# A hybrid attention layer on one core: the first softmax item a unit later, squares on ScalarE, three more short products

## The chip, the cores and the metric

The kernel runs on one core of a Trainium2 chip. A core has five engines that work through queues of their own, each in order: TensorE (PE, matrix products and transposes), VectorE (DVE), ScalarE (ACT), GpSimd (POOL) and SyncE (SP, which issues the loads). The metric is the device time of one execution in microseconds (us).

## The reference

One decoder layer for 256 positions and 1024 channels, all in float32. Two token mixers read one projection of the normalised input; their gated sum is projected and added to x; then a second norm and a gated feed-forward network with a causal convolution.

```
h = rmsnorm(x, g_mix)
q_a, kv_a, gate_a, qkv_b, merge = split(h @ w_in)          # 1024 x 5656
kc, vc = compress(...)                                     # small MLP with gelu over blocks of keys, values
o_a = nsa_attention(q_a, kc, vc, ks, vs, kw, vw, gate_a)   # 8 heads: compressed, selected, window
o_b = dilated_attention(qkv_b)                             # 12 heads in 3 groups
mixed = sigmoid(g_A) * (o_a @ w_proj_nsa) + sigmoid(g_B) * (o_b @ w_proj_dil)
x = x + mixed @ w_out
h = x * rsqrt(mean(x * x) + eps) * g_ffn                   # the second norm
x = x + (gelu(conv(h @ w_u)) * (h @ w_gate)) @ w_down
return rmsnorm(x, g_final)
```

## The kernel before

**Units.** The weights come in 64 units, mostly of 128 x 2048 float32, one load each into one of three `raw` buffers. A product in float32 is made of three products in a shorter format: ACT copies a unit to its high half `whi` (`split_hi`, L128), DVE subtracts to get the low half `wlo` (`split_lo`, L132), and the moving operand is split in the same way (`hTh`, `hTl`). `parts` (L162) first issues high by high and high by low, product by product (L177), and then low by high (L182): 32 and 16 products of 256 columns in a usual unit. The next load into a raw buffer waits until its low half is made.

**The order** is written out by hand, unit by unit, in the loop at L1094; there is no scheduler. Units 0 to 4 make keys, values and the queries of the first mixer, 5, 7 and 9 queries of the second, 6 and 8 the first layer of the compression MLP (L425), 10 to 15 its keys and values, 16 to 23 the merge gates, 24 to 26 the two projections, 27 to 30 `w_out`, and from unit 31 (`NFIRST`) on the feed-forward network.

**Items.** The softmax of the mixers is cut into items that are spread over the units (`slots`, L1085). An item in slot n makes its scores behind the products of unit n (`qk`, for the first mixer L850 and L852). During unit n+1 DVE adds the penalty and takes the row's extreme (`sm`, L864), ACT takes the exponential and its sum (L869), and DVE scales by one over the sum and a gate (`sm2`, three small operations and L883). Behind unit n+1 PE transposes the scaled scores (`tr`, L892, eight transposes), both engines copy them out (`te`, L897 and L898), and behind unit n+2 they multiply the values (`pv`, L905). Within a unit the loop writes `sm`, then the gelu of the compressed keys (`cmp_gelu`, only in unit 10, L751 to L762), then the low half of the next unit, then `sm2`; in unit 9 alone `sm2` goes ahead of the low half (L1109). The compressed keys are folded behind unit 9 (`cmp_fold`, L745).

**The second norm.** Each of the units 27 to 30 adds a quarter of `w_out`'s result to x (`ev_out`, L552): DVE adds (L555), ACT and DVE split the scaled result for the next products (`split_x`, L201 and L202), and POOL squares it and keeps a running sum of 128 x 2 x 256 (L561, L563), which it folds to `acc2` at the last quarter (L567). The column sums of `acc2` are taken on PE in unit 32 (L209), and the rest of the norm goes into the eviction of the feed-forward products. At unit 31 ACT's queue issues the load of the last gain into memory that the sums have held, so it waits for L567, and the high half of unit 33 stands behind it.

**Short products.** In units 24 and 33 `rt["kick"] = "own"` puts a product of 64 columns in front of the unit (L172), into columns that the first full product overwrites.

Of the kernel before, what the change touches and what calls it, by code (L numbers as in the profile page):

```python
# [14 lines left out]
AF = mybir.ActivationFunctionType  # L15
OP = mybir.AluOpType
# [77 lines left out]
def build(ctx, tc, a, out):  # L94
    nc = tc.nc
    V, A, P, T = nc.vector, nc.scalar, nc.gpsimd, nc.tensor
# [41 lines left out]
    def hi_of(i):  # L138
        if 2 <= i < len(units):
            split_tiles(units[i])  # L140
            (units[i].split or (split_hi, split_lo))[0](units[i])

    def lo_of(i):
        if 2 <= i < len(units):
            if i == 27:
                split_lo(units[i], 1024, 2048, P)
                return
            if i in SHARED:
                split_lo(units[i], 0, SHARED[i])
                split_lo(units[i], SHARED[i], 2048, P)  # L150
                return
            (units[i].split or (split_hi, split_lo))[1](units[i])
# [47 lines left out]
    def split_x(kt, x, g):  # L200
        A.activation(hTh[:, kt], x, AF.Copy, scale=g[:, kt:kt + 1])  # L201
        V.scalar_tensor_tensor(hTl[:, kt], x, g[:, kt:kt + 1], hTh.bitcast(F32)[:, kt],  # L202
                               op0=OP.mult, op1=OP.subtract)
# [45 lines left out]
    def mixer_tiles():  # L249
        M["QS"] = att.tile([128, 8, S], F32R, name="QS", tag="QS")  # L250
        for n in ("qb", "kb"):
            M[n] = att.tile([128, 6, S], F32, name=n, tag=n)
        M["vb"] = att.tile([128, 2, 3, 256], F32, name="vb", tag="vb")
# [3 lines left out]
    rt = {}  # L257
# [45 lines left out]
    def xc_tile():  # L303
        xr["XC"] = att.tile([128, 4, 520], F32R, name="XC", tag="MB")
        for i in range(4):
            V.memset(xr["XC"].bitcast(F32)[:, i, 512:520], 0.0)
# [19 lines left out]
    def split_cmp(i):  # L326
        f, XC = xr["f"][:, 2 * i:2 * i + 2], xr["XC"]
        hi, lo = XC[:, 2 * i:2 * i + 2, 0:256], XC[:, 2 * i:2 * i + 2, 256:512]
        A.activation(hi, f, AF.Copy)
        V.tensor_sub(lo, f, XC.bitcast(F32)[:, 2 * i:2 * i + 2, 0:256])  # L330
# [221 lines left out]
    def ev_out(c):  # L552
        def f(u):
            x = xT[:, 2 * c:2 * c + 2]
            V.tensor_tensor(out=x, in0=x, in1=u.p, op=OP.add)  # L555
            for k in range(2):
                split_x(2 * c + k, xT[:, 2 * c + k], G2)
            if c == 0:
                rt["sqs"] = att.tile([128, 4, 2, S], F32, name="sqs", tag="MA")
            sq = rt["sqs"][:, c]  # L560
            P.tensor_tensor(out=sq, in0=x, in1=x, op=OP.mult)  # L561
            if c:
                P.tensor_tensor(out=sq, in0=sq, in1=rt["sq"], op=OP.add)  # L563
            rt["sq"] = sq
            if c == 3:
                rt["acc2"] = const.tile([128, S], F32, name="acc2")
                P.tensor_tensor(out=rt["acc2"], in0=sq[:, 0], in1=sq[:, 1], op=OP.add)  # L567
        return f

    for c in range(4):  # L570
        units.append(Unit(2048, mm_out(c), ev_out(c)))
# [87 lines left out]
    NFIRST = len(units)  # L659
# [73 lines left out]
    def cmp_sum():  # L733

        S2 = att.tile([64, 2, 128], F32, name="S2", tag="c1")
        p = rt["ph"][0:64]
        A.activation(S2, p[:, :, 0], AF.Copy)
        V.tensor_tensor(out=S2, in0=p[:, :, 1], in1=S2, op=OP.add)
        cmp_["S2"] = S2
# [7 lines left out]
    def cmp_gelu():  # L747

        w = att.tile([128, 3, 64], F32, name="gl")
        x, y, e = w[:, 0], w[:, 1], w[:, 2]  # L750
        A.activation(x, cmp_["cm"][:, 0:64], AF.Copy)  # L751
        V.tensor_tensor(out=y, in0=x, in1=x, op=OP.mult)
        V.tensor_scalar(y, y, 0.044715, 1.0, op0=OP.mult, op1=OP.add)
        V.tensor_tensor(out=y, in0=y, in1=x, op=OP.mult)
        V.tensor_scalar(y, y, -50.0, None, op0=OP.max)
        A.activation(e, y, AF.Exp, scale=-2.0 * float(np.sqrt(2.0 / np.pi)))
        V.tensor_scalar(e, e, 1.0, None, op0=OP.add)
        V.reciprocal(e, e)
        hk = att.tile([128, 32], F32, name="hk")
        hv = att.tile([128, 4, 32], F32, name="hv")  # L760
        V.tensor_tensor(out=hk, in0=x[:, 0:32], in1=e[:, 0:32], op=OP.mult)
        V.tensor_tensor(out=hv, in0=x[:, None, 32:64].to_broadcast([128, 4, 32]),  # L762
                        in1=e[:, None, 32:64].to_broadcast([128, 4, 32]), op=OP.mult)
        cmp_["hk"], cmp_["hv"] = hk, hv
# [249 lines left out]
    def load_to(n):  # L1014
        nonlocal loaded
        while loaded < min(n, len(units)):
            load_unit(units[loaded])
            loaded += 1
# [63 lines left out]
    tables_pool3()  # L1082

    items = {11: [Cmp()]}
    slots = [8, 10] + list(range(12, 22))  # L1085
    seq = [c(h, t) for c in (Nsa, Dil) for q in (0, 2) for h, t in (((q,), 1), ((q + 1,), 1), ((q, q + 1), 0))]
    for n, it in zip(slots, seq):
        items.setdefault(n, []).append(it)
# [1 line left out]
    def at(i):  # L1090
        return items.get(i, [])

    post = []
    for i, u in enumerate(units):  # L1094
        load_to(i + LA)
        if i == 9:
            cmp_sum()
        for it in at(i - 3):
            it.fin()
        for it in at(i - 2):  # L1100
            it.te()
        for it in at(i - 1):
            it.sm()
        if i == 10:
            cmp_gelu()
        if i == 2:
            hi_of(3)
            lo_of(3)
        if i == 9:  # L1109
            for it in at(i - 1):  # L1110
                it.sm2()
        if i > 2:
            lo_of(i + 1)
        if i != 9:
            for it in at(i - 1):
                it.sm2()
        if i == 14:
            nc.sync.dma_start(xT, a["xT"])
        if i == 3:
            hi_of(5)  # L1120
            mixer_tiles()
            xc_tile()
            split_cmp(0)
            split_cmp(1)
            u1.evac(u1)
        if i == 4:
            split_keys()
        if i == 11:
            cmp_kv_ev()
        if i == 14:  # L1130

            ob = att.tile([128, 4, S], F32R, name="ob", tag="qa")
            OB.update(h=ob[:, 0:2], l=ob[:, 2:4])
        if i in (23, 24):
            m = ML[i - 23]
            A.activation(m, m, AF.Sigmoid)
        if i == NFIRST:
            st.close()
            ffn["pool"] = ctx.enter_context(tc.tile_pool(name="ffn", bufs=1))
            gf = ffn["pool"].tile([128, D], F32, name="gf")  # L1140
            nc.scalar.dma_start(gf, bass.AP(tensor=a["g_final"].tensor, offset=a["g_final"].offset,
                                            ap=[[0, 128], [1, D]]))
            X = ffn["pool"].tile([128, 2, D], F32, name="X")
            sq = ffn["pool"].tile([128, 512], F32, name="sq")
        if 24 <= i <= 25:
            hi_of(i + 2)
        if i in (24, NFIRST + 2):
            rt["kick"] = "own"
        u.mm(u)
        if not 24 <= i <= 26 and i > 1 and i != 3:  # L1150
            hi_of(i + 2)
        if i == 2:
            u0.evac(u0)
        if i == NFIRST + 1:
            rt["R2"] = rows_of(rt["rs2"], "R2", "o")
            units[NFIRST].evac(units[NFIRST])
            ps2 = pd([2, 512], "s")
            pt = [pd([512], "t"), pd([512], "t"), ps2[:, 0], ps2[:, 1]]
            for q in range(4):
                for c in range(4):  # L1160
                    T.transpose(pt[q][:, c * 128:c * 128 + 128], xT[:, 4 * (q % 2) + c, q // 2 * 128:q // 2 * 128 + 128],
                                ident)
            for q in range(4):
                A.activation(X[:, q // 2, q % 2 * 512:q % 2 * 512 + 512], pt[q], AF.Copy)
        if post:
            post.pop()()
        if u.pre:
            u.pre(u)
        if u.evac and i not in (0, 1, NFIRST):
            u.evac(u)  # L1170
        if i in (6, 7):
            q_parts(i - 6)
        if i == 7:
            gates_of()
        if u.pre:
            post.append(post_g(len([q for q in units[:i] if q.pre])))
        for it in at(i - 2):
            it.pv()
        for it in at(i - 1):
            it.tr()  # L1180
        for it in at(i):
            it.qk()
        if i == 9:
            cmp_fold()
        if i == 10:
            cmp_kv()
# [34 lines left out]
    x = X[:, 1, 768:1024]  # L1221
# [28 lines left out]
```

## Time and profile before

| | us |
|---|---|
| median of 3 executions (406.04 to 407.66) | 406.07 |
| the profiled execution | 406.5 |
| its span, first to last instruction | 404.7 |
| PE busy | 394.7 (98%) |
| DVE busy | 291.2 (72%) |
| ACT busy | 212.4 (52%) |
| POOL busy | 31.2 (8%) |

PE is busy almost all the time, and its granted clock is at full speed from the first slices to the last one of the page. Since a busy PE hides little, the thing to read is where it waits, and what stands in the queue of the engine that it waits for. Ends of products are modelled in the trace, their starts are measured.

### The profile page before, as it was taken

Reading aid. Unit: us, or ns where it says so; the run is one execution under the profiler, and the core shown is the slowest. Engines: PE = TensorE matmul, PEld = TensorE weight load, DVE = VectorE, ACT = ScalarE, POOL = GpSimd, SP = SyncE. Lnnn points to the kernel's source line nnn. Section 1 sums busy time; section 2 is a strip of 40 time slices with the busy share of each in tenths; the row PEclk is TensorE's granted clock in tenths of the full one; section 3 lists DMA queues with packets and bytes.
Section 4 is the critical chain, followed back from the end, with each engine's and each line's share of the span. In section 5 each row is a group of like instructions: output and inputs, shape, how many; then the busy total and the mean of one; then the engine's idle time right before and its main releaser. Section 6 shows DMA issues by size and latency. Waiting matters only on the chain.

```text
span 404.7 us, 8015 instructions
## 1 busy us (share of the span) xinstructions
PE 394.7 (98%) x3412; PEld 383.2 (95%) x3412; DVE 291.2 (72%) x486; ACT 212.4 (52%) x293; POOL 31.2 (8%) x58
## 2 busy tenths in 40 slices
PE   8999989999999999999999999999999999999993
PEld 6999989999998989999999999999999999999992
DVE  5879889887786557458897499676594774946853
ACT  5776764366664345663554765445264352643512
POOL 7100000000000000061143000000000000000012
PEclk9999999999999999999999999999999999999997
DMA  8965746345332532343556346662734726438002
GB/s 319 390 251 207 249 168 209 105 158 220 144 105 105 201 113 105 131 181 108 206 208 235 130 136 236 255 222 108 296 119 194 266 99 261 160 152 299 15 0 105
DMA packets 10980, 72.59 MB, mean 179 GB/s; under 512 B 1216, under 2 KB 1472, under 8 KB 2880
## 3 DMA queue, kind: packets, MB, share of 16 engines
q1 hardware_dynamic: 10512, 70.96, 48.2%
q10 hardware_dynamic: 432, 1.11, 0.7%
q8 instruction: 27, 0.44, 0.4%
q14 instruction: 9, 0.07, 0.1%
HBM read 71.02 MB, written 1.05 MB: 178 GB/s over the span
## 4 chain that ended last, share of the span: by engine, by line
PE 83%; DVE 10%; ACT 2%; DMA 2%; issue 1%; SPq 0%; POOLq 0%; POOL 0%; ACTq 0%
PE ps_d L177 25%; PE ps_d L182 12%; PE ps_o L177 9%; PE ps_s L630 8%; PE ps_t L630 7%; PE ps_o L182 5%; DVE wlo L132 4%; DMA first<-in_first_dram 2%; PE ps_t L177 2%; DVE hTl L202 2%; PE ps_d L344 2%; PE ps_o L905 2%; PE ps_s L946 1%; PE ps_t L892 1%; PE ps_d L280 1%
## 5 line engine op out<-in xcount | busy, mean ns | idle before, releaser
L132 DVE TENSOR_TENSOR wlo<-raw,whi 128x2048 fp32r<-128x2048 f32 (+2 forms) x61 | 135.2, 2217 | 4.2 <-ACT whi L128 4.2
L128 ACT ACTIVATE whi<-raw 128x2048 fp32r<-128x2048 f32 (+1 forms) x61 | 114.8, 1883 | 33.6 <-DMA raw<-in_wts_dram 28.8
L177 PE MATMUL ps_d<-hTh,whi 128*128 128x256 f32 x384 | 90.1, 280 | 0.0
L177 PE MATMUL ps_d<-hTl,whi 128*128 128x256 f32 x384 | 89.0, 277 | 0.0
L177 PEld LDWEIGHTS ps_d<-hTh,whi 128*128 128x128 f32 x384 | 72.2, 188 | 1.7 <-issue 1.3
L177 PEld LDWEIGHTS ps_d<-hTl,whi 128*128 128x128 f32 x384 | 72.2, 188 | 0.0
L182 PE MATMUL ps_d<-hTh,wlo 128*128 128x256 f32 x384 | 47.8, 277 | 0.0
L182 PEld LDWEIGHTS ps_d<-hTh,wlo 128*128 128x128 f32 x384 | 45.7, 188 | 0.0
L177 PE MATMUL ps_o<-hTh,whi 128*128 128x256 f32 x160 | 36.9, 277 | 0.0
L177 PE MATMUL ps_o<-hTl,whi 128*128 128x256 f32 x160 | 36.8, 276 | 0.0
L585 ACT ACTIVATE C<-U,small 128x256 f32<-128x256 f32 x22 | 12.0, 595 | 44.1 <-DVE U L581 44.1
L177 PEld LDWEIGHTS ps_o<-hTl,whi 128*128 128x128 f32 x160 | 30.1, 188 | 0.0
L177 PEld LDWEIGHTS ps_o<-hTh,whi 128*128 128x128 f32 x160 | 30.0, 188 | 0.0
L589 DVE SCALAR_TENSOR_TENSOR C<-U,small,C 128x256 f32<-128x256 f32 x44 | 19.4, 482 | 7.5 <-ACT C L585 7.4
L869 ACT ACTIVATE E<-E,ast 128x256 f32<-128x256 f32 (+1 forms) x32 | 14.2, 444 | 13.4 <-DVE ast L864 13.4
L581 DVE TENSOR_TENSOR U<-ps_d,R 128x512 f32<-128x512 f32 x6 | 4.1, 690 | 23.0 <-PE ps_d L182 19.2
L182 PE MATMUL ps_o<-hTh,wlo 128*128 128x256 f32 x160 | 19.8, 276 | 0.0
L132 POOL TENSOR_TENSOR wlo<-raw,whi 128x1024 fp32r<-128x1024 f32 x3 | 7.7, 2579 | 154.8 <-ACT whi L128 154.8
L182 PEld LDWEIGHTS ps_o<-hTh,wlo 128*128 128x128 f32 x160 | 18.9, 188 | 0.0
L581 DVE TENSOR_TENSOR U<-ps_o,R 128x512 f32<-128x512 f32 x5 | 3.4, 689 | 17.6 <-PE ps_o L182 17.6
L1207 POOL TENSOR_TENSOR tiny<-cst,tiny 128x1 f32<-128x1 f32 x2 | 1.4, 696 | 170.6 <-ACT sq L1206 170.6
L366 DVE TENSOR_TENSOR ML<-ps_d,R 128x512 f32<-128x512 f32 x8 | 5.5, 692 | 12.3 <-PE ps_d L182 12.3
(269 smaller groups left out, 762.5 us busy)
## 6 DMA issues: line engine op xcount, KB each, us to landing
raw<-in_wts_dram SPq DMA_DIRECT2D x61, 1024.0 KB, 4.8
first<-in_first_dram SPq DMA_DIRECT2D x2, 768.0 KB, 8.1
raw<-in_wts_dram SPq DMA_DIRECT2D x1, 1120.0 KB, 11.0
xn<-in_xn_dram SPq DMA_DIRECT2D x2, 512.0 KB, 12.4
xT<-in_xT_dram SPq DMA_DIRECT2D x1, 1024.0 KB, 6.9
first<-in_first_dram SPq DMA_DIRECT2D x2, 384.0 KB, 5.3
gf<-in_g_final_dram ACTq DMA_DIRECT2D x1, 512.0 KB, 3.7
out_dram<-X SPq DMA_DIRECT2D x1, 512.0 KB, 2.6
```

The costliest lines, as they stand in the source:

```text
L128: A.activation(u.hi[:, u.o + c0:u.o + c1], u.raw[:, c0:c1], AF.Copy)
L132: (eng or V).tensor_sub(u.lo[:, u.o + c0:u.o + c1], u.raw[:, c0:c1], u.hi.bitcast(F32)[:, u.o + c0:u.o + c1])
L177: T.matmul(po, l, r, start=start and bank not in banks, stop=False, skip_group_check=True)
L182: T.matmul(po, l, r, start=False, stop=stop and n == len(ks) - 1, skip_group_check=True)
L202: V.scalar_tensor_tensor(hTl[:, kt], x, g[:, kt:kt + 1], hTh.bitcast(F32)[:, kt], op0=OP.mult, op1=OP.subtract)
L344: T.matmul(u.p[:, i], l[:, kt, i * 128:i * 128 + 128], r[:, kt], start=kt == 0 and i == 0 and q == 0, stop=kt == 7 and q == 2, skip_group_ ...
L581: V.tensor_tensor(out=U[:, :, 2:], in0=u.p, in1=bc(rt["R2"], 2), op=OP.mult)
L585: A.activation(C[:, c], U[:, c, 2:], AF.Identity, scale=CW(2, t), bias=CB[:, t:t + 1])
L589: V.scalar_tensor_tensor(C[:, c], U[:, c, w:w + S], CW(w, t), C[:, c], op0=OP.mult, op1=OP.add)
L630: T.matmul(ffn["y"][t][ch][:, b:e] if own is None else own, x[:, kt, t * 128:t * 128 + 128], w[:, kt, ch * 512 + b:ch * 512 + e], start=st ...
L869: A.activation(self.E[:, i], self.E[:, i], AF.Exp, bias=mn[:, i:i + 1], scale=-1.0, accum_out=dn[:, i:i + 1])
L905: T.matmul(oA[js[c]][g * 64:g * 64 + 64, t * 128:(t + 1) * 128], Vn[:, k, b * 128 + g * 64:b * 128 + g * 64 + 64], self.PT[:, i], start=t ...
```

## The change

Three edits. The first item of the first mixer moves from slot 8 to slot 9; all other items stay. The squares of the second norm are made by ACT instead of POOL; POOL keeps the running sum over the first three quarters, folds it to `acc2` at the third, and at the last quarter adds the two halves of that quarter's squares to `acc2`, one after the other. And units 11, 13 and 23 get a short product in front as well.

```diff
             sq = rt["sqs"][:, c]
-            P.tensor_tensor(out=sq, in0=x, in1=x, op=OP.mult)
-            if c:
+            A.activation(sq, x, AF.Square)
+            if c in (1, 2):
                 P.tensor_tensor(out=sq, in0=sq, in1=rt["sq"], op=OP.add)
             rt["sq"] = sq
-            if c == 3:
+            if c == 2:
                 rt["acc2"] = const.tile([128, S], F32, name="acc2")
                 P.tensor_tensor(out=rt["acc2"], in0=sq[:, 0], in1=sq[:, 1], op=OP.add)
+            if c == 3:
+                for k in range(2):
+                    P.tensor_tensor(out=rt["acc2"], in0=rt["acc2"], in1=sq[:, k], op=OP.add)
...
-    slots = [8, 10] + list(range(12, 22))
+    slots = [9, 10] + list(range(12, 22))
...
-        if i in (24, NFIRST + 2):
+        if i in (11, 13, 23, 24, NFIRST + 2):
             rt["kick"] = "own"
```

Lines behind the second edit stand three lines further down in the changed kernel. On PE, before, from the end of unit 8 (L425) to the start of unit 11; the 32 products L177 of each unit are left out. The scores stand ahead of unit 9, the transposes behind it, and `pv` and the second item's scores behind unit 10:

```order
L425 MATMUL ps_d<-wlo,XC 64x256 x8
L850 MATMUL ps_s<-KH,QS 128x512 x2
L852 MATMUL ps_s<-KL,QS 128x512 x2
...
L182 MATMUL ps_d<-hTh,wlo 128x256 x16
L892 MATMUL ps_t<-ident,E 128x128 x8
L745 MATMUL ps_o<-E_142,S_746 128x32 x2
...
L905 MATMUL ps_o<-PT,Vn 64x128 x8
```

And of the change, the same stretch up to the short product of unit 11:

```order
L425 MATMUL ps_d<-wlo,XC 64x256 x8
...
L182 MATMUL ps_d<-hTh,wlo 128x256 x16
L853 MATMUL ps_s<-KH,QS 128x512 x2
L855 MATMUL ps_s<-KL,QS 128x512 x2
L748 MATMUL ps_o<-E_142,S_741 128x32 x2
...
L895 MATMUL ps_t<-ident,E 128x128 x8
...
L772 MATMUL ps_o<-hk,small 64x32 x2
L773 MATMUL ps_o<-small,hv 128x64
L172 MATMUL ps_d<-hTh,whi 128x64
```

The scores moved behind unit 9 and the transposes behind unit 10; `pv` of this item is now behind unit 11.

On DVE, before, the operations of the first item between the compression's sum (L738) and the gelu (L752 on); the four reductions L864 alternate with readings of their accumulators:

```order
L738 TENSOR_TENSOR S_746<-ps_d,S_746 64x256
L864 ISA E,ast<-ps_s,tab 128x256
...
L876 TENSOR_SCALAR ast<-ast 128x4
L877 RECIPROCAL ast<-ast 128x4
L880 TENSOR_TENSOR ast<-ast,gates 128x4
L883 TENSOR_SCALAR E<-E,ast 128x256 x4
L132 TENSOR_TENSOR wlo<-raw,whi 128x2048
L454 SCALAR_TENSOR_TENSOR qb<-ps_d,scB,R 128x256 x2
L898 COPY PT<-ps_t 128x512
L752 TENSOR_TENSOR gl<-gl 128x64
```

Of the change, from the same sum to the scaling:

```order
L741 TENSOR_TENSOR S_741<-ps_d,S_741 64x256
L132 TENSOR_TENSOR wlo<-raw,whi 128x2048
L454 SCALAR_TENSOR_TENSOR qb<-ps_d,scB,R 128x256 x2
L867 ISA E,ast<-ps_s,tab 128x256
...
L755 TENSOR_TENSOR gl<-gl 128x64
...
L765 TENSOR_TENSOR hv<-gl 128x128
L132 TENSOR_TENSOR wlo<-raw,whi 128x2048
L879 TENSOR_SCALAR ast<-ast 128x4
...
L886 TENSOR_SCALAR E<-E,ast 128x256 x4
```

Between the reductions and the scaling now stand the gelu chain of eight operations (L755 to L765) and the low half of unit 11. On ACT the copy that begins the gelu chain (L754, before L751) stands behind the item's four exponentials.

On POOL, the second norm, both orders in one piece; `acc` is `acc2`:

```order
-L561 TENSOR_TENSOR sqs<-xT 128x512
-L563 TENSOR_TENSOR sqs<-sqs 128x512
-L567 TENSOR_TENSOR acc_2583<-sqs 128x256
+L563 TENSOR_TENSOR sqs<-sqs 128x512 x2
+L567 TENSOR_TENSOR acc_2524<-sqs 128x256
+L570 TENSOR_TENSOR acc_2524<-acc_2524,sqs 128x256 x2
 L215 TENSOR_TENSOR tiny<-tiny,cst 128x2
```

The multiplies are gone from POOL, the fold comes ahead of the last quarter, and two adds of 128x256 follow it. Each of the four activations (L561) stands on ACT behind the two copies L201 of its quarter and ahead of the next high half.

## Rows read from the trace of the kernel before

**Rows 1.** Who waited for whom on PE, from 17 to 235 us.
```profile
PE ps_t L892 <- DVE E L883: 0.9, 1, 0.9
PE ps_d L280 <- DVE wlo L132: 0.4, 1, 0.4
```

**Rows 2.** Time line of PE, units 9 and 10: start, length, instructions, [idle before].
```profile
54.74 1.98 PE L182 MATMUL ps_d<-hTh,wlo 128*128 128x256 f32 x16
57.62 1.46 PE L892 MATMUL ps_t<-ident,E 128*128 128x128 f32 x8 [0.90 <-DVE E L883]
59.01 0.63 PE L745 MATMUL ps_o<-E,S 64*128 64x32 f32 x4
59.57 0.39 PE L177 MATMUL ps_d<-hTh,whi 128*128 128x256 f32 x1
...
65.23 1.09 PE L905 MATMUL ps_o<-PT,Vn 128*64 128x128 f32 x16
```

**Rows 3.** Chain that ended last, unit 11 and behind it: start, length, work.
```profile
68.05 3.82 PE ps_d L177 x32
...
73.76 0.87 PE ps_t L892 x8
```

**Rows 4.** Time line of DVE during units 9 and 10.
```profile
53.94 0.41 DVE L864 CUSTOM_DVE_ANT_0 E<-ps_s,tab 128x256 f32<-128x256 f32 x1
...
56.51 0.17 DVE L876 TENSOR_SCALAR ast<-ast 128x4 f32<-128x4 f32 x1 [1.12 <-ACT E L869]
...
57.12 1.14 DVE L883 TENSOR_SCALAR E<-E,ast 128x256 f32<-128x256 f32 x4
58.17 2.29 DVE L132 TENSOR_TENSOR wlo<-raw,whi 128x2048 fp32r<-128x2048 f32 x1
60.38 0.87 DVE L454 SCALAR_TENSOR_TENSOR qb<-ps_d,scB,R 128x256 f32<-128x256 f32 x2
...
61.76 0.22 DVE L752 TENSOR_TENSOR gl<-gl 128x64 f32<-128x64 f32 x1
...
64.15 2.28 DVE L132 TENSOR_TENSOR wlo<-raw,whi 128x2048 fp32r<-128x2048 f32 x1
```

**Rows 5.** Time line of ACT: first exponential, copy ahead of the gelu.
```profile
54.39 0.51 ACT L869 ACTIVATE E<-E,ast 128x256 f32<-128x256 f32 x1 [2.22 <-DVE ast L864]
...
59.68 0.22 ACT L751 ACTIVATE gl<-ps_o 128x64 f32<-128x64 f32 x1 [0.40 <-PE ps_o L745]
```

**Rows 6.** Time lines of DVE, POOL, ACT and PE around the second norm.
```profile
197.87 1.28 DVE L202 SCALAR_TENSOR_TENSOR hTl<-xT,small,hTh 128x256 fp32r<-128x256 f32 x2 [0.58 <-ACT hTh L201]
...
213.80 2.25 DVE L202 SCALAR_TENSOR_TENSOR hTl<-xT,small,hTh 128x256 fp32r<-128x256 f32 x2 [0.58 <-ACT hTh L201]
215.98 2.83 DVE L132 TENSOR_TENSOR wlo<-raw,whi 128x2048 fp32r<-128x2048 f32 x1
...
214.42 1.35 POOL L563 TENSOR_TENSOR sqs<-sqs 128x512 f32<-128x512 f32 x1
215.85 0.80 POOL L567 TENSOR_TENSOR acc<-sqs 128x256 f32<-128x256 f32 x1
...
217.12 1.92 ACT L128 ACTIVATE whi<-raw 128x2048 fp32r<-128x2048 f32 x1 [2.95 <-POOL acc L567]
...
217.34 1.07 PE L280 MATMUL ps_d<-hTh,whi 128*128 128x256 f32 x8
218.86 1.19 PE L280 MATMUL ps_d<-hTh,wlo 128*128 128x256 f32 x8 [0.45 <-DVE wlo L132]
...
220.80 0.50 PE L209 MATMUL ps_o<-cst,acc 128*128 128x1 f32 x4
```

**Rows 7.** Chain that ended last, unit 33, which has a short product.
```profile
226.45 3.73 PE ps_o L177 x32
```

**Rows 8.** Windows: us, busy PE PEld DVE ACT POOL, granted clock, DMA share, GB/s.
```profile
397.80:400.40 2.60, 0.00 (x0) 0.00 (x0) 1.67 (x5) 1.32 (x3) 1.24 (x3) 1.00 0.17 69
400.50:404.70 4.20, 0.00 (x0) 0.00 (x0) 0.47 (x1) 0.53 (x1) 0.00 (x0) 0.50 0.50 196
```

## The prediction

> **What bounds the kernel now.** I first asked who waits for whom on TensorE (PE) between the start-up and the first up-projections. There are only two waits [rows 1]: 0.9 us for the scaled scores E, 0.4 us for a low half wlo. In the rest of that stretch PE runs one product behind the other, so whatever the change adds in front of a product that waits, or takes from it, goes to the end of the kernel in full. Then I read PE's, VectorE's (DVE's) and ScalarE's (ACT's) time lines around the first wait, and DVE's, GpSimd's (POOL's) and PE's around the second, since the change touches just these two places.
>
> First wait [rows 2]. The 16 low products of unit 9 start at 54.74 and issue every 0.113 us (1.98 us for all, of which the last one's own 0.28), so PE is free at 56.55. The eight transposes of the first softmax item start at 57.62, 1.07 us later, and they take 1.39 us to the fold L745 at 59.01, because the four scalings of E come one by one. Eight transposes that find their data ready take 0.87 us (at 73.76 [rows 3]). So the first item costs 1.07 + 0.52 = **1.59 us** today.
>
> Second wait [rows 6]. In unit 32 eight products start at 217.34; the next eight could start 8 x 0.113 us later, at 218.25, and start at 218.86, when wlo of that unit is done; the second of them comes 0.1 us late as well. That is **0.7 us**.
>
> **The first item a unit later.** Nothing is added or removed, items are only handed to unit 9 instead of unit 8. The scores are now made behind unit 9, the softmax runs during unit 10 and the transposes stand behind unit 10. So the old loss of 1.59 us goes. The question is whether E is ready when unit 10 ends.
>
> When PE gets there: all its work up to the end of unit 10 is what it was, less the transposes and less the wait. Unit 10 ended at 65.23 [rows 2], so now 65.23 - 1.39 - 1.07 = 62.77. The scores end 0.56 us (the fold, 59.01 to 59.57) before unit 10 starts, which is at 59.57 - 2.46 = 57.1; so at 56.55.
>
> When DVE gets there, in the new order of its queue, which it works through in order:
> - At 53.94 [rows 4] it was free and began the first reduction (L864). Now the low half of unit 10 comes first: 2.21 us (58.17 to 60.38), to 56.15.
> - The eviction of unit 9 takes 0.8 (0.87 with its tail, at 60.38), to 56.95. The scores are there by then.
> - Four reductions, and ACT's four exponentials behind them: the first exponential started 0.45 us after the first reduction (53.94, 54.39 [rows 4, 5]), and 2.1 us later DVE could go on (56.51). So the exponentials run from 57.4 to 59.4.
> - The gelu chain of the compressed keys now stands between them and the scaling. It begins with a copy on ACT (0.22 us [rows 5]), which in ACT's queue stands behind the four exponentials: DVE gets it at 59.65, after an idle 1.3 us. The chain, with its own round trip through ACT, took from 61.76 to 64.15, 2.39 us: 62.04.
> - Then the low half of unit 11, 2.21 us: 64.25. Only then the three small operations (56.51 to 57.12, 0.61 us) and the scalings, from 64.86.
> - The transposes ended 1.89 us after the first scaling began (57.12 to 59.01): 66.75.
>
> So PE waits at the new place from 62.77 to about 65.3, and with slow transposes loses 66.75 - 62.77 - 0.87 = **3.1 us**, instead of 1.59. The special branch for unit 9, which puts the scaling ahead of the low half, no longer finds an item; for unit 10 the low half goes first. Net **+1.5 us**. Behind it the queue on DVE is the eviction of unit 10, the copy of the transposes and the next item's reductions; moving all of these by what PE is late gives no second wait. The product of probabilities and values moves from ahead of unit 11 to behind it, the same length. Loads come no later: the low half of unit 10, which frees a raw buffer, ends at 56.15 instead of 60.4. Bounds: +1.2 if the gelu chain, whose idle 0.3 us was measured behind a busy DVE, closes up; +1.9 if each of the three hand-overs between ACT and DVE costs 0.13 us more than I read off. I take +1.5, the value of the rows themselves.
>
> **The squares.** Four multiplies leave POOL and become four activations of 128x512 on ACT, an estimated 0.6 to 0.7 us each (an exponential of half that width takes 0.51 [rows 5], a high half of four times 1.92); one add of 128x512 is replaced by two of 128x256. ACT has the room: it stood idle for 2.95 us ahead of 217.12 [rows 6]; in the three quarters before, the activation only moves a high half that isn't wanted until the quarter after.
>
> What it does to DVE: the pair of hTl operations at 213.80 takes 2.25 us while POOL's multiply and add run to 215.77 (214.42 + 1.35), and 1.28 us at 197.87, where POOL has only a multiply; the low half at 215.98 takes 2.83, while POOL's last add runs to 216.65, against 2.29 without POOL [rows 4, 6]. The pair ends 0.28 us after POOL's add (216.05 and 215.77): DVE is held up until POOL is through, not slowed in proportion. The Trainium skill says the same (SBUF — State Buffer, "Who interferes with whom": the pair of ports is an exclusive lock, and issue order decides who blocks); the trace agrees for POOL first. By proportional sharing the saving would be smaller; by the lock it is all of the overlap.
>
> Without the multiply and the add, the pair ends by 213.80 + 1.28 = 215.1 at the latest, and the low half by 217.4. PE wants it at 218.25, so 0.85 us is spare. What is left of POOL in this quarter is two adds of 0.80 us, behind the activation, from about 214.3 to 214.8. If DVE's low half gets in first, POOL waits to about 216.5 and is through at 218.1 to 219.0; its sum is wanted at 220.80 less 0.7, and the high half of unit 33, whose queue waits for it, by 226.4 [rows 7]. If POOL gets in first, the low half ends at 218.2 to 218.4, and PE waits 0.2 us at most. I take **-0.7 us**, bounds -0.75 and -0.4, and 0 for the rival below.
>
> **The short products.** Unit 11's first 32 products take 3.82 us [rows 3], those of unit 33, which has such a product in front, 3.73 [rows 7]; the 16 behind follow at the same pace, so a unit that comes into the faster pace saves about 0.13 us, and the short product costs one more issue, at least 0.11 us like any other [rows 2]. Three units: **-0.1 us**; if the pace doesn't change, +0.35; if all three come out like the fastest units, -0.3.
>
> **Sum.** +1.5 - 0.7 - 0.1 = +0.7 us. The profiled execution took 406.5 us (404.7 of span, 1.8 around it), 0.4 above the median 406.07; the sum gives it 407.2, and the median **406.8 us**.
>
> **The rivals.**
> 1. *The clock falls in the new wait.* PE idles for 2.5 us and then runs only a few short transposes until 66.75. At the end of the run PE does nothing from 397.8 on; the granted clock is 1.00 up to 400.4 and 0.50 from 400.5 [rows 8]: 2.4 GHz, then 1.2, after PE had stood idle for 2.6 us. The new gap is about that long; the old one of 1.07 us did not do it. How long the lower level would stay the trace shows only from below, 4.2 us to the end; that many microseconds at half pace cost 2.1 us. Time 406.8 + 2.1 = 408.9, slower by 0.7%. It decides if the idle time with the thin transposes behind it counts like the idle time at the end of the run. The Trainium skill has a rule for it (TensorE: Matmul & The Clock Gate, "HAM oscillation — how this bites in real kernels": a wait of PE that is long enough throttles the clock, and the next products start at half rate); by this rule a gap of this kind is in danger, and no wait in this trace is long enough to test it. Chance 0.24.
> 2. *The new wait doesn't appear.* If the scaling were ready at 62.8, the old 1.59 us would be gone for nothing: -1.59 - 0.7 - 0.1 = -2.4 us, 403.7 us, faster by 0.6%. For that DVE would have to reach the scaling 2 us earlier than its queue allows, with the gelu chain or the low half of unit 11 finished elsewhere. Against it: both stand ahead of the scaling in the queue. Chance 0.1.
> 3. *The squares give nothing back*, because POOL's remaining adds hold up DVE as long as before, or PE's wait only moves to hTl: +1.4 us, 407.5. Chance 0.12.
>
> **How the numbers follow.** The forecast, a new wait of 3.1 us and a lost wait of 0.7, has a chance of 0.54; its own range, with the bounds of the terms (+1.2 to +1.9, -0.75 to -0.4, -0.3 to +0.35), is 406.2 to 407.9. What tells from no change here is 0.5%, 2.0 us: the forecast and the third rival lie within it, the first rival ends above, the second below. Faster 0.1, within 0.66, slower 0.24. The range goes from 404.9, which leaves out the second rival and takes in half of its way, to 409.0, which takes in the first.
>
> **What would show it.** After: no wait behind unit 9; a wait of PE for E of 2 to 3 us behind unit 10, with the scalings on DVE at about 64.9 and the gelu chain from about 59.7; unit 12 starting about 1.5 us later than 76.3; hTl pairs of about 0.9 us in place of 2.25; no wait in unit 32; the first 32 products of units 11, 13 and 23 in about 3.73 us. The prediction is wrong if the scaling is there when unit 10 ends, or if the granted clock has a gap near 66 us.

## The result and the profile after

| | before | after |
|---|---|---|
| median of all runs, us | 406.07 | 408.13 |
| lowest and highest of 12, us | 405.81 to 407.66 | 407.09 to 411.47 |
| profiled execution, us | 406.5 | 408.03 |
| its span, us | 404.7 | 406.2 |
| its mean granted clock | 0.995 | 0.992 |

The change makes the kernel 0.62% slower: the ratio to before is 1.0062, 95% interval 1.0047 to 1.0077. The forecast was 406.8 within 404.9 to 409.0; the time lies in the range, but above the forecast's own 406.2 to 407.9: it is the first rival that came.

Two waits stood in the view of who waits for whom on PE, from 17 to 235 us [rows 1]. After, in the same stretch, one is left (us in total, times, longest):

```profile
PE ps_t L895 <- DVE E L886: 2.3, 2, 2.2
```

It is the wait for the scaled scores, at its new place and more than twice as long; the wait for unit 32's low half is gone. The time line of PE at the new place, the end of unit 10:

```profile
60.60 1.98 PE L182 MATMUL ps_d<-hTh,wlo 128*128 128x256 f32 x16
64.73 0.33 PE L895 MATMUL ps_t<-ident,E 128*128 128x128 f32 x1 [2.15 <-DVE E L886]
65.26 1.59 PE L895 MATMUL ps_t<-ident,E 128*128 128x128 f32 x7 [0.19 <-DVE E L886]
66.50 1.20 PE L853 MATMUL ps_s<-KH,QS 128*128 128x512 f32 x2
67.50 1.05 PE L855 MATMUL ps_s<-KL,QS 128*128 128x512 f32 x2
```

The low products issue until 62.41 (60.60 + 16 x 0.113); the first transpose starts at 64.73, 2.3 us later. Then look at starts: from 64.73 to 66.50 eight transposes take 1.77 us, and the four score products take 2.0 us (66.50 to 68.49), where the next item's four took 1.1 in the kernel before, behind the same unit. The score products have become about half as fast. The windows tell why (us, busy PE, PEld, DVE, ACT, POOL, granted clock, DMA share, GB/s):

```profile
62.50:64.70 2.20, 0.08 (x1) 0.00 (x0) 2.10 (x6) 0.00 (x0) 0.00 (x0) 1.00 0.00 0
64.70:65.40 0.70, 0.47 (x2) 0.28 (x3) 0.70 (x4) 0.00 (x0) 0.00 (x0) 1.00 0.70 117
65.50:68.90 3.40, 3.40 (x16) 2.47 (x14) 1.56 (x3) 0.60 (x1) 0.00 (x0) 0.51 0.64 270
69.00:74.90 5.90, 5.90 (x53) 5.77 (x53) 5.56 (x20) 3.89 (x9) 0.00 (x0) 1.00 0.22 74
```

PE idles in the first window, runs two transposes in the second, and then the granted clock is at its lower level, 1.2 GHz in place of 2.4, until about 69. What DVE did meanwhile:

```profile
56.45 0.41 DVE L867 CUSTOM_DVE_ANT_0 E<-ps_s,tab 128x256 f32<-128x256 f32 x1
...
59.12 0.23 DVE L755 TENSOR_TENSOR gl<-gl 128x64 f32<-128x64 f32 x1 [1.22 <-ACT gl L754]
...
61.52 2.29 DVE L132 TENSOR_TENSOR wlo<-raw,whi 128x2048 fp32r<-128x2048 f32 x1
63.72 0.16 DVE L879 TENSOR_SCALAR ast<-ast 128x4 f32<-128x4 f32 x1
...
64.33 1.14 DVE L886 TENSOR_SCALAR E<-E,ast 128x256 f32<-128x256 f32 x4
```

That is the queue as forecast: reductions, an idle 1.22 us until ACT's copy, the gelu chain from 59.12 to 61.52, the low half, the small operations, the scaling. Between the end of the reductions and the scaling stand 4.6 us (59.12 to 63.72) that E doesn't need.

The second norm after, on DVE, POOL and PE:

```profile
205.55 2.28 DVE L132 TENSOR_TENSOR wlo<-raw,whi 128x2048 fp32r<-128x2048 f32 x1
...
215.63 0.89 DVE L202 SCALAR_TENSOR_TENSOR hTl<-xT,small,hTh 128x256 fp32r<-128x256 f32 x2 [0.58 <-ACT hTh L201]
216.43 2.29 DVE L132 TENSOR_TENSOR wlo<-raw,whi 128x2048 fp32r<-128x2048 f32 x1
...
222.50 2.29 DVE L132 TENSOR_TENSOR wlo<-raw,whi 128x2048 fp32r<-128x2048 f32 x1 [3.78 <-ACT whi L128]
...
205.71 3.28 POOL L563 TENSOR_TENSOR sqs<-sqs 128x512 f32<-128x512 f32 x1 [19.92 <-ACT sqs L561]
...
216.66 3.47 POOL L570 TENSOR_TENSOR acc<-acc,sqs 128x256 f32<-128x256 f32 x2 [1.41 <-ACT sqs L561]
223.20 2.16 POOL L215 TENSOR_TENSOR tiny<-tiny,cst 128x2 f32<-128x2 f32 x1 [3.07 <-ACT tiny L214]
...
224.65 1.10 PE L280 MATMUL ps_d<-hTl,whi 128*128 128x256 f32 x8
225.59 0.61 PE L222 MATMUL ps_o<-ident,tiny 128*128 128x128 f32 x4
```

The pair of hTl operations takes 0.89 us instead of 2.25, the low half 2.29 instead of 2.83 [rows 6], and PE runs on. POOL now is the one that is held up: each of its pieces that starts behind DVE's low half ends only after it (205.71 + 3.28 = 208.99, the low half at 207.83; 216.66 + 3.47 = 220.13, the low half at 218.72), while the low halves keep their 2.28 and 2.29 us. L215, two columns wide, takes 2.16 us under the low half of 222.50; before, with no low half beside it, it took 0.72:

```profile
221.67 0.72 POOL L215 TENSOR_TENSOR tiny<-tiny,cst 128x2 f32<-128x2 f32 x1 [5.02 <-ACT tiny L214]
```

After, L215 ends at 225.36, and PE wants it at 225.59: the norm's tail has 0.2 us to spare.

Set end to end: unit 8 starts at 47.71 (48.19 before) and unit 12 at 78.52 (76.18), so +2.82 us between them, 1.5 of them, as the second experiment below shows, from the clock; -0.74 between the first L280, the start of unit 31 (214.16, 211.90 before), and L222 (225.59, 224.07). With the 0.48 us that this execution was ahead of the other at unit 8, which no edit explains, that is +1.6; the span grew by 1.5.

### The profile page after: what moved, and what is told of

Read it like the earlier page. It is cut to its first block, busy times and chain, and to the rows that moved or that the text cites. A ratio compares the mean times of both kernels' runs of the same rounds, so it can differ in the third digit from the quotient of the medians.

```text
span 406.2 us, 8021 instructions
## 1 busy us (share of the span) xinstructions
PE 395.3 (97%) x3415; PEld 383.7 (94%) x3415; DVE 286.9 (71%) x486; ACT 214.6 (53%) x297; POOL 33.9 (8%) x55
## 4 chain that ended last, share of the span: by engine, by line
PE 91%; DVE 4%; DMA 2%; ACT 1%; issue 1%; SPq 0%; POOLq 0%; POOL 0%; ACTq 0%
PE ps_d L177 25%; PE ps_d L182 12%; PE ps_o L177 12%; PE ps_s L633 8%; PE ps_t L633 7%; PE ps_o L182 6%; PE ps_d L280 3%; PE ps_t L177 2%; DMA first<-in_first_dram 2%; PE ps_t L895 2%; PE ps_d L344 2%; DVE wlo L132 2%; PE ps_o L908 2%; PE ps_s L949 1%; PE ps_o L546 1%; PE ps_t L978 1%
## 5 line engine op out<-in xcount | busy, mean ns | idle before, releaser
L177 PE MATMUL ps_d<-hTh,whi 128*128 128x256 f32 x384 | 89.8, 280 | 0.0
L177 PE MATMUL ps_d<-hTl,whi 128*128 128x256 f32 x384 | 88.8, 277 | 0.0
L177 PEld LDWEIGHTS ps_d<-hTh,whi 128*128 128x128 f32 x384 | 72.2, 188 | 1.6 <-issue 1.3
L177 PEld LDWEIGHTS ps_d<-hTl,whi 128*128 128x128 f32 x384 | 72.2, 188 | 0.0
L177 PE MATMUL ps_o<-hTh,whi 128*128 128x256 f32 x160 | 36.9, 277 | 0.0
L177 PE MATMUL ps_o<-hTl,whi 128*128 128x256 f32 x160 | 36.8, 276 | 0.0
L177 PEld LDWEIGHTS ps_o<-hTl,whi 128*128 128x128 f32 x160 | 30.1, 188 | 0.0
L177 PEld LDWEIGHTS ps_o<-hTh,whi 128*128 128x128 f32 x160 | 30.0, 188 | 0.0
```

What stands on the lines that cost most here:

```text
L177: T.matmul(po, l, r, start=start and bank not in banks, stop=False, skip_group_check=True)
```

## The experiments

All kernels are the one before or the changed one with the edit shown. The times of before beside them are 406.1 to 406.4.

**The edits alone.** Slot 9 alone (`slots = [9, 10] + ...`), the squares alone (the hunk of `ev_out`), the short products alone (`if i in (11, 13, 23, 24, NFIRST + 2)`).

> The kernel before with the first item moved to slot 9, nothing else. Theory A (the scaling stands behind the gelu chain and a low half on VectorE, so TensorE loses 3.1 us behind unit 10 in place of 1.59 behind unit 9, and in this wait the clock may fall, worth another 1.3): a wait of 2.2 us for E, span +1.5 us where the clock holds and +2.8 where it falls once; about 408.8 us. Theory B (the item's move is neutral, the time is lost in the other two edits): within 0.3 us of 406.07.

> The kernel before with the squares on ScalarE and the sums of three quarters, nothing else. Theory A: the wait of unit 32 (0.7 us) is gone, 405.4 us, granted clock as before. Theory B (GpSimd's adds, locked out behind the low halves, make something later wait): 406.1 us or more, with a wait of TensorE at the norm's sums or rows.

> The kernel before with the short products of units 11, 13 and 23, nothing else. Theory A: their units fall into the faster pace (0.113 us a product in place of 0.118), 0.1 us each saved less the short product: 405.9 us, not to be told from before. Theory B (short products cost their issue and change nothing): 406.4 us.

Measured: slot alone 408.94 (407.4 to 409.08), ratio 1.006 (1.0048 to 1.0072); squares alone 405.25 (404.94 to 407.21), 0.9977 (0.9964 to 0.999); short products alone 405.82 (405.68 to 406.1), 0.999 (0.9981 to 0.9999). So the slot is the loss; the squares give a little, and the short products at most a little. The waits on PE with the slot alone:

```profile
PE ps_t L892 <- DVE E L883: 2.4, 2, 2.2
PE ps_d L280 <- DVE wlo L132: 0.5, 1, 0.5
```

and its clock, in windows as above:

```profile
62.80:65.00 2.20, 0.04 (x1) 0.00 (x0) 2.10 (x6) 0.00 (x0) 0.00 (x0) 1.00 0.00 0
...
65.80:69.10 3.30, 3.30 (x15) 2.44 (x13) 1.42 (x3) 0.60 (x1) 0.00 (x0) 0.50 0.68 283
```

The same wait and the same fall, without the other edits. One of its five executions shows a mean clock of 0.995 and took 407.4; the four others, at 0.991 and 0.992, took 408.4 to 409.1.

The squares' profile brought a surprise at the old place, where E is 0.9 us late as before:

```profile
56.50:57.40 0.90, 0.05 (x1) 0.00 (x0) 0.80 (x5) 0.90 (x1) 0.00 (x0) 1.00 0.99 419
57.40:59.50 2.10, 1.92 (x13) 1.49 (x13) 2.10 (x4) 1.30 (x2) 0.00 (x0) 1.00 0.14 59
59.70:63.00 3.30, 3.30 (x17) 3.30 (x17) 2.87 (x9) 0.47 (x3) 0.00 (x0) 0.50 0.43 146
63.10:66.00 2.90, 2.90 (x27) 2.90 (x27) 2.87 (x4) 1.53 (x1) 0.00 (x0) 1.00 0.45 184
```

Behind the old wait and the thin transposes the clock falls too, in this execution. It took 407.21, as another with a mean clock of 0.990 took 407.09; the eight at 0.994 to 0.998 took 404.94 to 405.68. The kernel before has such executions as well (407.45 and 407.67 at 0.990, 408.23 at 0.992, beside 22 of 405.81 to 406.91 at 0.994 to 0.998); none of these three was profiled, so where the clock fell in them is not shown. The old wait, then, is not too short to touch the clock; as far as the mean clocks tell, the longer one does it in most executions, the shorter one in some.

**Is the wait the loss, or the clock behind it?** Eighteen products of 256 columns, extra work, fill the wait in the changed kernel; they write columns that the transposes overwrite.

```diff
+                if self.js == (0,) and self.t == 1 and q == 0:
...
+                    for n in range(18):
+                        T.matmul(pf[:, 0:256], wh[:, n % 8, 0:128], hTh[:, n % 8], start=True, stop=True,
...
```

> The changed kernel with 18 extra products of 256 columns (2.0 us of TensorE's time, into columns that the transposes overwrite) between unit 10 and the transposes. Theory A (part of the loss is the clock that falls in the idle wait): the transposes start as before, but the granted clock stays at 1.00 through 62 to 70 us, and the runs lie at 407.1 us, where those of the changed kernel without a fall lie; none above 408. Theory B (the spread of the changed kernel comes from something else): the same spread, 407.1 to 411, as without the products.

Measured: 407.48 (406.68 to 408.82), ratio 1.0031 (1.0016 to 1.0046). The same windows as for the changed kernel:

```profile
62.50:64.70 2.20, 2.20 (x20) 2.01 (x18) 2.10 (x6) 0.00 (x0) 0.00 (x0) 1.00 0.00 0
...
65.50:68.90 3.40, 3.40 (x27) 2.83 (x27) 2.89 (x12) 1.67 (x6) 0.00 (x0) 1.00 0.68 282
```

E comes at the same time, but the clock stays, in this window and by the mean clock in all 12 executions (0.994 to 0.998):

```profile
64.83 0.33 PE L901 MATMUL ps_t<-ident,E 128*128 128x128 f32 x1
...
66.13 0.72 PE L853 MATMUL ps_s<-KH,QS 128*128 128x512 f32 x2
...
67.25 0.31 PE L772 MATMUL ps_o<-hk,small 128*64 128x32 f32 x4
```

Unit 12 starts at 77.14, 29.34 us behind the start of unit 8 (47.80), instead of 30.81 in the changed kernel and 27.99 before. That divides the loss at this place, from one execution of each kernel: **+1.35 us for the item, +1.47 for the clock**. It comes out of the starts too: transposes 0.47 (1.77 against 1.30), scores 0.87 (1.99 against 1.12), the small products behind them 0.15. Half of the 3.4 us at the low level would be 1.7; the transposes, which in part wait for the scalings at any clock, may be the difference.

The twelve executions fall into two groups, though, 406.68 to 406.88 and 408.07 to 408.82, at the same clock, where none above 408 was expected. The clock doesn't make the upper group; a second effect, below, has about this size, but no execution of this group was profiled.

**Can the scaling be early?** In the changed kernel the item's scaling is put ahead of unit 10's gelu chain and low half, or only ahead of the low half; a third kernel has slot and early scaling without the other two edits. The edit of the first, where the added lines stand in front of `cmp_gelu()` under `if i == 10:`; in the second `if i == 9:` becomes `if i == 10:` instead:

```diff
+            for it in at(i - 1):
+                it.sm2()
...
-        if i == 9:
-            for it in at(i - 1):
-                it.sm2()
...
-        if i != 9:
+        if i != 10:
```

> The changed kernel with the three small operations and the scaling of the first item ahead of the gelu chain and the low half in VectorE's queue. Theory A: E is ready at about 61, before unit 10 ends at 62.3, no wait of TensorE is left there and the clock holds: 1.59 + 0.7 + 0.1 less than before, 403.7 us. Theory B (the gelu chain or the low half, now later, makes TensorE wait at the keys or in unit 11): 404.7 us or more, with that wait in the trace.

> The changed kernel with the scaling of the first item behind the gelu chain but ahead of the low half of unit 11. Theory A (TensorE waits for as long as the queue ahead of the scaling is): the scaling begins 2.2 us earlier, at 62.1, the transposes at 62.6, a wait of 0.2 to 0.3 us is left and the transposes are slow; 0.7 us more than with the scaling ahead of the chain, no fall of the clock: 405.0 us. Theory B (the gelu chain alone, not the low half, makes the wait): a wait of 1.5 us or more stays.

> The kernel before with the item in slot 9 and the scaling ahead of the gelu chain, without the other two edits. Theory A: the old loss of 1.59 us is gone and nothing takes its place: 404.5 us. The runs of the kernel with all edits fell into a group at 404 and one at 406 that isn't explained; if the squares or the short products bring the second group, it is missing here; if the earlier stage does, about four in ten runs lie 2 us higher.

Measured: ahead of both 404.42 (403.65 to 406.51), ratio 0.997 (0.9953 to 0.9986); ahead of the low half 404.9 (404.38 to 406.44), 0.9974 (0.996 to 0.9987); ahead of both, without squares and short products, 404.84 (404.74 to 405.43), 0.9961 (0.9946 to 0.9975). The first two kernels fall into two groups again, 403.65 to 404.42 and 405.79 to 406.51, 404.38 to 404.96 and 405.91 to 406.44; their medians mix them. Time lines of DVE and PE in the first of them:

```profile
58.90 0.17 DVE L879 TENSOR_SCALAR ast<-ast 128x4 f32<-128x4 f32 x1 [1.11 <-ACT E L872]
...
59.52 1.15 DVE L886 TENSOR_SCALAR E<-E,ast 128x256 f32<-128x256 f32 x4
...
62.97 2.28 DVE L132 TENSOR_TENSOR wlo<-raw,whi 128x2048 fp32r<-128x2048 f32 x1
...
62.26 1.03 PE L895 MATMUL ps_t<-ident,E 128*128 128x128 f32 x8
63.05 0.72 PE L853 MATMUL ps_s<-KH,QS 128*128 128x512 f32 x2
```

E is scaled at 60.7, 1.6 us before PE wants it; the eight transposes take 0.79 us, without any wait, and the low half of unit 11, now until 65.25, is still there in time for its products from about 68.5. With the scaling only ahead of the low half 0.2 us of the wait are left. So later slot and early scaling belong together: the slot without the scaling costs 0.6%, with it gains 0.4%.

**The second norm without the early fold.** Squares on ScalarE, but POOL adds all four quarters and folds at the end, as before.

> The kernel before with the squares on ScalarE, but the sum kept over all four quarters and folded at the end, as before. Theory A (VectorE's low halves and GpSimd's adds lock each other out, first come first served): GpSimd's last add of 512 columns waits for the low half of unit 32, the fold ends near 221, the high half of unit 33 and the square root behind it come later, and TensorE waits for the norm's rows: about 1 us more than with three quarters, 406.2 us. Theory B (GpSimd's end doesn't matter): 405.3 us as with three quarters.

Measured: 405.83 (405.52 to 407.28), ratio 0.9987 (0.9976 to 0.9999), half a microsecond more than with the sums of three quarters, where 1 us was expected; the intervals of the two ratios overlap. POOL and the waits on PE:

```profile
214.09 3.21 POOL L563 TENSOR_TENSOR sqs<-sqs 128x512 f32<-128x512 f32 x1 [2.23 <-ACT sqs L561]
...
220.67 2.68 POOL L215 TENSOR_TENSOR tiny<-tiny,cst 128x2 f32<-128x2 f32 x1 [2.55 <-ACT tiny L214]
...
PE ps_t L892 <- DVE E L883: 0.9, 1, 0.9
PE ps_o L222 <- POOL tiny L215: 0.2, 1, 0.2
```

The add lies behind DVE's low half whether it is one of 512 columns or two of 256, but it is followed by one more fold, and the norm's tail, which has 0.2 us to spare in the changed kernel, now is 0.2 us late in this view. By starts it costs more: from the start of unit 31 (211.60) to the short product in front of unit 33 (225.62) PE takes 14.02 us here and 13.54 with the sums of three quarters (213.35 to 226.89). The 0.48 us are about the difference of the times.

**The two groups.** The kernel with the scaling only ahead of the low half was profiled in its upper group, at 406.07. The chain that ended last, in its units 28 and on, and the same of the version without the added short products, described below, at 403.87:

```profile
194.25 3.77 PE ps_o L177 x32
...
225.16 0.03 PE ps_o L172
225.19 3.85 PE ps_o L177 x32
...
247.88 0.94 PE ps_s L633 x8
```

```profile
193.85 3.63 PE ps_o L177 x32
...
223.79 0.03 PE ps_o L172
223.82 3.73 PE ps_o L177 x32
...
245.69 0.94 PE ps_s L633 x8
```

Products of the same shape, none waiting, clock at full speed, but 118 ns apart instead of 113, from the last products of unit 27 (`w_out`, L546) on until L633 comes: 53.63 us against 51.84, **1.8 us**, which is about the distance of the groups. Two kernels tried what makes it: the changed kernel with early scaling and without the three added short products, and the same with these and a fourth in front of unit 28.

> The changed kernel with the item's scaling ahead of unit 10's gelu chain and low half, and without the three added short products (units 24 and 33 keep theirs). It asks what brings the two groups of runs, 403.65 to 404.42 and 405.79 to 406.51, that the same kernel had with them. Theory A, the added short products make TensorE's slow pace of the later units more likely (the slot and scaling alone, without them and without the squares on ScalarE, had 404.74 to 405.43 and no upper group): one group, at about 404.84 - 0.7 for the squares = 404.1 to 404.8. Theory B, the upper group comes from the squares or by chance: two groups again, the lower at 404.0 to 404.5 and the upper some 2 us above, at 406 to 406.6.

> The changed kernel with the item's scaling ahead of unit 10's gelu chain and low half, and a fourth added short product, in front of unit 28, right behind the place where a profile showed the slow pace begin (118 ns a product from the end of unit 27, 3.77 us for 32 products in place of 3.63). Theory A, a short product ends the slow pace: no run in the upper group, all at 403.6 to 404.5. Theory B, it doesn't (the one in front of unit 33 did not end it there): two groups, 403.7 to 404.5 and 405.8 to 406.5, as without it.

Measured: without the short products 404.32 (403.87 to 405.47), ratio 0.9947 (0.9928 to 0.9965), five executions up to 404.57 and one at 405.47; with the fourth 404.85 (404.28 to 405.23), 0.9954 (0.9935 to 0.9972). Neither shows the upper group, which the two kernels with early scaling and the three short products had in four of 9 and five of 12, and the kernel with the filler in six of 12. That speaks for the short products as a part of the cause, but doesn't settle it: six executions are few, and the kernel before with the short products alone has none of its 11 executions (405.68 to 406.1) in such a group, so they don't bring it by themselves; and one of 29 executions of the kernel before, which has none of the three, took 407.36 at a mean clock of 0.994. With the fourth, four of six executions lie above the 404.5 that was expected. Its own profile, of one at 405.23:

```profile
194.22 0.03 PE ps_o L172
194.25 3.85 PE ps_o L177 x32
...
225.14 0.03 PE ps_o L172
225.17 3.73 PE ps_o L177 x32
```

It did not end the slow pace in front of unit 28 (32 products in 3.85 us); the one in front of unit 33 did (3.73), which in the profile above it did not. So a short product can end it and can fail to; what decides stays open. From the start of unit 28 to that of unit 33 this execution is 1.0 us behind the one without the added ones (30.92 against 29.94), about half of the distance of the groups. The version without the added ones has the lowest median that was run, but the intervals overlap.

## Why the prediction came out as it did

**The step that failed is the clock.** The sum has no term for it: the text put the chance that it falls at 0.24 and argued that the old wait "did not do it". It falls in the profiles of the changed kernel and of the slot alone, filling the wait keeps it, and the text's own sign of being wrong, a gap of the granted clock near 66 us, came (65.5 to 68.9). The argument took one execution of the kernel before for all: with the squares alone a profile shows the fall behind the old wait, and three of 25 executions of the kernel before have as low a mean clock. The Trainium skill tells of such a fall (TensorE: Matmul & The Clock Gate, "HAM oscillation — how this bites in real kernels": a long wait throttles the clock, and the next products start at half rate); the trace agrees in the half rate, 0.51 after 2.2 us of idle PE and a few transposes, but with shorter waits than those of the page's case, 2.2 us and 0.9. The first rival had the right mechanism; its price, 2.1 us, was too high: the 4.2 us taken for the time at the low level were 3.4, and of these 1.47 were lost. That 408.13 lies in the range is owed to the range, which was drawn wide enough to take in this rival, and not to the sum.

**The item** was right: the wait has the place, the length (2.3 us for 2.5) and the queue behind it that were forecast, each step on DVE 0.5 us early, as is unit 8. Net +1.35 for +1.5; the transposes that get their data one by one took 1.30 us at the full clock, behind the filler, not 1.39.

**The squares** were right: -0.74 in the trace for -0.7, DVE's operations at their own lengths again; the time fell by 0.0023 of 406, 0.9 us, with an interval of 0.4 to 1.5. POOL's remaining adds came out by the first of the two orders given, DVE's low half first. POOL is through at 220.13; since PE starts unit 31 2.26 us later than before, that is 217.87 on the forecast's time line, a little earlier than the 218.1 to 219.0 given. PE took the column sums at 222.32 without a wait. The third rival is excluded.

**The short products** give next to nothing, as the -0.1 said: unit 11's 32 products take 3.72 us behind 0.12 for the short one, where they took 3.85 by starts before. From unit 8 to unit 31 the kernel with these products alone takes 163.75 us (47.59 to 211.34), the kernel before 163.71 (48.19 to 211.90). The -0.4 us of the runs has an interval of 0 to -0.8 and is not found in the trace.

**The second rival** was rightly set aside for this change, and its condition rightly named: the kernel with the scaling ahead of gelu chain and low half is that case, and takes 404.42, with a lower group of 403.65 to 404.42, for the 403.7 it gave.

**Sum.** The executions of the changed kernel whose mean clock is 0.995 took 407.09 and 407.27, near the base forecast of 406.8; those at 0.992 and 0.993 took 407.97 to 408.23, about the 1.47 us above 406.8. One at 408.52 has a clock of 0.998: it would fit the slow pace, but was not profiled. Four of 409.68 to 411.47 show 0.986 to 0.989, lower than one fall gives (3.4 us at half the clock are an estimated 0.004 of the mean over 406 us); perhaps it falls twice there, which no profile shows.

## What to carry to other kernels

Before an item is moved to a later slot, read what stands ahead of it in the queue of the engine that makes it ready: here the move was worth 0.4% only together with the scaling's own move ahead of 4.6 us of work that it didn't need. A wait of the matrix engine that ends in thin work can cost more than its length: price the clock as a term of the sum, and look at the mean clock of several executions of the kernel before, not at one profile, to see whether a wait touches it. When runs fall into two groups, profile one of each before a cause is named.

## What the runs showed of the hardware

- Back-to-back products of 128x256 have two steady paces, 113 and 118 ns, at a full clock and without a wait; either lasts over several units (51.84 and 53.63 us for the same stretch) until something else comes between, and a product of 64 columns in front of a unit sometimes changes it.
- The granted clock can fall to its lower level for 3.4 us after 0.9 us of idle PE with eight transposes, four small products and the first of a unit behind it (profile of the squares alone), and after 2.2 us with two transposes behind it (changed kernel, slot alone). By the mean clocks it does so in some executions of one and the same kernel with the short wait (two of 10 with the squares alone, perhaps 3 of 25 of the kernel before) and in most with the long one (four of five with the slot alone). With products in the long wait it did so in none of 12.
- An operation on POOL that starts just behind DVE's low half takes 3.2 to 3.3 us where it took 1.35 [rows 6], and one of two columns 2.16 or 2.68 where it took 0.72, while the low half keeps its 2.28: the lock that held DVE up behind POOL before now holds POOL behind DVE. The Trainium skill has it so (SBUF — State Buffer, "Who interferes with whom": the shared pair of ports is an exclusive lock); the trace agrees in both directions.
